# Query blocks of a PEER layer: lo parts on GpSimd, activation copies spread over the blocks, two blocks fed by the second norm

## The chip, the cores and the metric

The kernel runs on one core of a Trainium2 chip. The core's engines run side by side, each through its own list of instructions in order, and wait for each other by semaphores: PE (TensorE) multiplies matrices, DVE (VectorE) and ACT (ScalarE) work element by element, POOL (GpSimd) so far only issues row gathers, and SP issues most of the other DMAs. The metric is the time of one execution on the device, in microseconds.

## The reference

One layer of a decoder block on 512 tokens of 1024 numbers, in float32. The change lies between the second norm and the search for experts:

```python
h2 = modulate(rmsnorm(x, norm2_g[l]), shift2, scale2)
x = x + gate2[:, None, :] * peer(h2, peer_wq[l], peer_subkeys[l], peer_u[l], peer_v[l])

def peer(h, wq, subkeys, u_tab, v_tab):
    xt = h.reshape(T, D)
    q = (xt @ wq).reshape(T, PEER_HEADS, 2, PEER_HALF)               # 16 blocks of 128 columns
    sc = jnp.einsum('thpd,hpkd->thpk', q, subkeys)
    vals, ids = lax.top_k(sc, PEER_TOPK)                             # 16 of 128
    ...                                                              # 16 of 256 sums, softmax
    u = jnp.take(u_tab, ic, axis=0); a = jnp.einsum('chkd,cd->chk', u, xc)
    wgt = gc * jax.nn.gelu(a)
    vv = jnp.take(v_tab, ic, axis=0); return jnp.einsum('chkd,chk->cd', vv, wgt)
```

## The kernel before

**Products in three parts.** A float32 matrix is split into hi, a rounded copy that ACT writes (line 176), and lo, the rest, which DVE writes as raw minus hi (line 177, `split`). A product is three matmuls a piece of 128 rows: hi by hi, hi by lo, lo by hi (lines 200 to 202, `mm3`); the third is the first that reads the weights' lo. A block of weights is 128 by 1024 numbers, so a block is 8 pieces and 24 matmuls. `weights_of` loads a block (`raw`, 5 buffers), and splits it; hi and lo have 4 buffers each, so the hi of block n+4 waits until PE has read that of block n.

**The second norm** gives its result in eight pieces (line 230 on ACT: fH, lines 229 and 231 on DVE: f and fL). Ahead of it x is turned by PE and written away in eight DMAs (line 536, `x1s<-xn`; three buffers for xn). The first query block, `early`, takes each piece as it comes. Then f is turned by 16 transposes (line 593) and copied out (hN and h2N, line 595), and ACT copies fH and fL, 352 columns of each piece, to h2H and h2L, 16 copies (line 598). h2H and h2L are what the dense blocks multiply with.

**Query blocks** 0 to 15: `query(hp)` multiplies and copies the result to qs (line 735); `scores(hp)` multiplies qs with the subkeys (line 742, psc), copies that to scd (line 744), and DVE takes the sixteen largest (`level1`, lines 631 to 636, three groups of tokens); after each second block also those of the sums (`level2`, lines 642 to 655). On PE the scores of block n stand behind the matmuls of block n+1.

**Dense blocks**, `first()`: u for 128 experts times all tokens (pa), 24 matmuls of 352 columns, with lo parts on DVE. They are called between the steps of `lookup`, where DVE turns found places into expert numbers (eq), and then between the steps of `build`, where it spreads the gates (B, line 946) for PE (gps, line 954).

The order on each engine is set when the program is built: a scheduling layer turns the calls into one list an engine. A tile's buffers and the semaphores follow from the pools.

Of the kernel before, what the change touches and what calls it, by code (L numbers as in the profile page):

```python
# [7 lines left out]
F32 = mybir.dt.float32  # L8
# [5 lines left out]
AF = mybir.ActivationFunctionType  # L14
# [8 lines left out]
DC = 8  # L23
# [3 lines left out]
TU = TD - HT  # L27
# [8 lines left out]
RING = 3  # L36
LOOK = 3
SPILL = 68
EARLY = 1
STB = 2  # L40
LD = 5
AHEAD = 7
# [47 lines left out]
def body(tc, p):  # L90
    nc = tc.nc
# [18 lines left out]
    def bank(name):  # L110
        return psm.tile([P, 512], F32, tag="m", name=name)
# [55 lines left out]
    mark = [None]  # L167

    def after(ins, mark):

        if mark is not None:
            tc.add_manual_dep(ins.ins, mark.ins.name, mybir.DependencyInfo(
                mybir.DependencyClass.Sync, mybir.DependencyReason.DATA), reason="pace")

    def split(h, l, f):
        nc.scalar.activation(h, f, AF.Copy)  # L176
        nc.vector.tensor_sub(l, f, h.bitcast(F32))  # L177

    def load(src):
        raw = ld.tile([P, D], F32, tag="ld", bufs=LD, name="raw")  # L180
        nc.sync.dma_start(raw, src)
        return raw

    def parts(src):

        raw = load(src)
        h = hl.tile([P, D], F32R, tag="h", bufs=4, name="hi")
        l = hl.tile([P, D], F32R, tag="l", bufs=4, name="lo")
        split(h, l, raw)
        return h, l  # L190

    def weights_of(src):

        h, l = parts(src.rearrange("p a b -> p (a b)"))
        return (lambda k: h[:, k * P:(k + 1) * P]), (lambda k: l[:, k * P:(k + 1) * P])

    def mm3(ps, w, rh, rl, ks=range(DC), k0=0, k1=DC - 1):
        wh, wl = w
        for k in ks:
            nc.tensor.matmul(ps, wh(k), rh(k), start=(k == k0), stop=False)  # L200
            nc.tensor.matmul(ps, wh(k), rl(k), start=False, stop=False)  # L201
            mark[0] = nc.tensor.matmul(ps, wl(k), rh(k), start=False, stop=(k == k1))  # L202
# [13 lines left out]
    def tmp(name):  # L216
        return tp.tile([P, T], F32, name=name, **T2)
# [59 lines left out]
    def some_weights(m):  # L277
        for b, w in zip(FIRST, WHEN):
            if w == m:
                wj[b] = weights_of(p["w_in"][b])  # L280

    some_weights(-1)
    for m, k in enumerate(ORDER):
        if k < DC - NR:
            ada((k, 8 + k))
        else:
            ps = ada_rows(m)
            for q in range(2):
                pick = rt.tile([P, P], F32, tag="pick", name="pick", bufs=1)
                nc.vector.scalar_tensor_tensor(pick, ps[:, q, :], 1.0, ident, op0=OP.mult, op1=OP.mult,  # L290
                                               accum_out=modv[:, q, k:k + 1])
        nc.vector.tensor_add(modv[:, 0:2, k], modv[:, 0:2, k], adabv[:, 0:2, k])
        nc.vector.scalar_tensor_tensor(s1[:, k:k + 1], mod[:, 8 + k:9 + k], 1.0, S("n1g", k), op0=OP.add, op1=OP.mult)
        f = tmp("f")
        nc.vector.tensor_mul(f, xT[:, k, :], r1)
        nc.scalar.activation(f, f, AF.Identity, scale=s1[:, k:k + 1], bias=mod[:, k:k + 1])
        split(hH[:, k, :], hL[:, k, :], f)
        some_weights(m)
        if m == 4:
            nc.sync.dma_start(cs2, p["cst"][:, KEEP:])  # L300
# [35 lines left out]
    def proj(b):  # L336
        w = weights_of(p["w_in"][b])
        ps = bank("pj")
        mm3(ps, w, hh, hlo)
        return ps  # L340
# [122 lines left out]
    def part_norm(ss, src, g, o):  # L463
        r = rstd(ss, 512)
        for k in range(4):
            f = tmp("f")
            nc.vector.scalar_tensor_tensor(f, src[:, k, :], S(g, k), r, op0=OP.mult, op1=OP.mult)
            split(mH[:, o + k, :], mL[:, o + k, :], f)
# [4 lines left out]
    def out_half(b, half):  # L473
        if half == 0:
            wo[b] = weights_of(p["w_out"][b])
            py[b] = bank("py")
        mm3(py[b], wo[b], mh, ml, range(4 * half, 4 * half + 4))
# [50 lines left out]
    def spill(half, when):  # L528
        for c in range(NCH):
            ps = bank("xt")  # L530
            for i in range(4):
                after(nc.tensor.transpose(ps[:, i * P:(i + 1) * P], xT[:, 4 * half + i, c * P:(c + 1) * P], ident),
                      when)
            xn = rt.tile([P, 512], F32, name="xn", **R2)
            nc.scalar.activation(xn, ps, AF.Copy)
            nc.sync.dma_start(x1s[c][:, half * 512:(half + 1) * 512], xn)
# [22 lines left out]
    h2H = pp.tile([P, DC, TU], F32R, name="h2H")  # L559
    h2L = pp.tile([P, DC, TU], F32R, name="h2L")  # L560
# [12 lines left out]
    fH = hx.tile([P, DC, T], F32R, name="fH")  # L573
    fL = hx.tile([P, DC, T], F32R, name="fL")
    r2 = rstd(ss2, D)
    spill(0, end)
    spill(1, end)
    early = [(weights_of(p["wq"][b]), bank("pq")) for b in range(EARLY)]
    fs = []
# [4 lines left out]
    for r, (dst, cs) in enumerate(((hN, slice(TD - P, TD)), (h2N, slice(TD, T)))):  # L584
        pg = [bank("pg0"), bank("pg1")]
        for k in range(DC):
            b = mod[:, 24 + k:25 + k]
            f = fs[k]
# [4 lines left out]
            nc.tensor.transpose(pg[k // 4][:, (k % 4) * P:(k % 4 + 1) * P], f[:, cs], ident)  # L593
        for k in range(2):
            nc.scalar.activation(dst[:, k * 512:(k + 1) * 512], pg[k], AF.Copy)
    for k in range(DC):
        for d, x in ((h2H, fH), (h2L, fL)):
            nc.scalar.activation(d[:, k, :], x[:, k, 0:TU].bitcast(F32), AF.Copy)

    xp_s.close()  # L600
    tp_s.close()
    r4, r4_s = pool("r4", side="right")
# [26 lines left out]
    def level1(sc, v, ids, mark=None):  # L629

        after(nc.vector.max(v[:, 0:8], sc), mark)
        nc.vector.max_index(ids[:, 0:8], v[:, 0:8], sc)
        rest = rt.tile([P, P], F32, tag="rest", name="rest", bufs=2)
        nc.vector.match_replace(rest, v[:, 0:8], sc, -3e38)
        nc.vector.max(v[:, 8:16], rest)
        nc.vector.max_index(ids[:, 8:16], v[:, 8:16], rest)  # L636

    def level2(h, n, R):

        cand = R["pool"].tile([P, n, 112], F32, tag=f"cand{n}", name="cand", bufs=1)  # L640
        V = R["V"][:, :, h]
        nc.vector.tensor_add(cand[:, :, 0:64].rearrange("p c (a b) -> p c a b", a=4),
                             V[:, :, 0, 0:4, None].to_broadcast([P, n, 4, 16]),
                             V[:, :, 1, None, :].to_broadcast([P, n, 4, 16]))
        nc.vector.tensor_add(cand[:, :, 64:112].rearrange("p c (a b) -> p c a b", a=12),
                             V[:, :, 0, 4:16, None].to_broadcast([P, n, 12, 4]),
                             V[:, :, 1, None, 0:4].to_broadcast([P, n, 12, 4]))
        pos = R["pos"]
        for c in range(n):
            v0, v1 = R["v"][:, c, h, 0:8], R["v"][:, c, h, 8:16]  # L650
            nc.vector.max(v0, cand[:, c, :])
            nc.vector.max_index(pos[:, c, h, 0:8], v0, cand[:, c, :])
            nc.vector.match_replace(cand[:, c, :], v0, cand[:, c, :], -3e38)
            nc.vector.max(v1, cand[:, c, :])
            nc.vector.max_index(pos[:, c, h, 8:16], v1, cand[:, c, :])
# [69 lines left out]
    def query(hp):  # L725
        sk = rp.tile([P, P], F32, tag="sk", name="sk", bufs=3)
        if hp < EARLY:
            ps = early[hp][1]
        else:
            w = weights_of(p["wq"][hp])  # L730
            ps = bank("pq")
            mm3(ps, w, lambda k: fH[:, k, :], lambda k: fL[:, k, :])
        nc.sync.dma_start(sk, p["sk"][hp])
        qs = tmp("qs")
        nc.scalar.activation(qs, ps, AF.Copy)
        return qs, sk

    def scores(hp, qs, sk):
        h, q = divmod(hp, 2)
        pc = bank("psc")  # L740
        for c in range(NCH):
            nc.tensor.matmul(pc[:, c * P:(c + 1) * P], qs[:, c * P:(c + 1) * P], sk, start=True, stop=True)
        sc = tmp("scd")[:, 0:TD].rearrange("p (c k) -> p c k", c=ND)
        nc.scalar.activation(sc, pc[:, 0:TD].rearrange("p (c k) -> p c k", c=ND), AF.Copy)
        nc.scalar.activation(scg[hp // 8][:, hp % 8, :], pc[:, TD:T], AF.Copy)
        for c in range(ND):
            level1(sc[:, c, :], Rd["V"][:, c, h, q], Rd["I"][:, c, h, q])
        if q:
            level2(h, ND, Rd)

    last = None
    for hp in range(16):
        now = query(hp)
        if last:
            scores(hp - 1, *last)
        last = now
    scores(15, *last)
    weights(ND, Rd)
# [373 lines left out]
```

## Time and profile before

| what | us |
|---|---|
| three runs | 1451.26, 1445.46, 1447.48; median 1447.48 |
| the profiled execution: its time, its span | 1445.51, 1443.6 |
| PE busy, DVE busy | 1391.7 (96%), 1242.0 (86%) |
| ACT busy, POOL busy | 616.1 (43%), 411.4 (29%) |

The span runs from the first to the last instruction of the profile; times of places are counted from its start. The time holds 1.9 us beside the span. The second norm lies at 230 to 252 us, the query blocks' matmuls at 240 to 350, the choice of their largest sums until 372, the first gates at 455. A row of the timeline reads: start, length, engine, line, operation, tile written from tiles read, sizes, count, and in brackets the engine's idle time before it and what ended that. The length of a pipelined instruction is longer than its step to the next.

### The profile page before, as it was taken

The numbers are of one execution on the slowest core, as the hardware profiler recorded it, in microseconds if no ns is written. First come the engines' busy times: TensorE is split into PE (matmuls) and PEld (weight loads), VectorE is DVE, ScalarE is ACT, GpSimd is POOL, SyncE is SP. The second block draws the span as 40 slices with busy tenths as digits, with TensorE's granted clock in tenths as the row PEclk, the third lists the DMA queues.
The fourth block names the chain that finished last, engine by engine and source line by source line (L and its number), as shares of the span: only waits on it lengthen the run. The fifth ranks groups of instructions, "written<-read, shape, count | busy, mean of one in ns | idle before, by whom it ended". The sixth has DMA issues, their size and how long they took to land.

```text
span 1443.6 us, 21238 instructions
## 1 busy us (share of the span) xinstructions
PE 1391.7 (96%) x7696; PEld 1222.1 (85%) x7696; DVE 1242.0 (86%) x2267; ACT 616.1 (43%) x1041; POOL 411.4 (29%) x292
## 2 busy tenths in 40 slices
PE   6999998999897999999999999999999999999998
PEld 4776776788897999999888888889999999889997
DVE  7778978799989999998668888888789988898964
ACT  4534646423633555464433434343343324333431
POOL 0000000000032330511034444446545546565400
PEclk9999999999998999999999999999999999999999
DMA  8645535222496997898999999999999999999843
GB/s 282 226 164 166 202 124 188 82 85 89 151 305 200 382 377 280 327 384 325 364 332 362 409 395 378 396 357 380 355 362 394 388 357 343 363 343 393 319 146 131
DMA packets 134377, 418.80 MB, mean 290 GB/s; under 512 B 12801, under 2 KB 39553, under 8 KB 132737
## 3 DMA queue, kind: packets, MB, share of 16 engines
q1 hardware_dynamic: 92800, 266.45, 51.1%
q0 software_dynamic: 41472, 151.01, 27.7%
q8 instruction: 60, 0.98, 0.3%
q14 instruction: 45, 0.36, 0.1%
HBM read 375.77 MB, written 41.62 MB: 289 GB/s over the span
## 4 chain that ended last, share of the span: by engine, by line
PE 63%; DVE 24%; DMA 5%; issue 5%; ACT 2%; POOL 1%; SPq 0%; DVEq 0%; ACTq 0%; POOLq 0%
PE o L997 11%; PE o L996 11%; PE o L998 11%; PE pa L200 6%; PE pa L202 6%; PE pa L201 6%; DVE lo L177 4%; DVE junk L213 2%; DVE B L946 2%; DVE junk L784 1%; PE py L200 1%; PE py L201 1%; DVE I L636 1%; PE py L202 1%; POOL row L776 1%
## 5 line engine op out<-in xcount | busy, mean ns | idle before, releaser
L176 ACT ACTIVATE hi<-raw 128x1024 fp32r<-128x1024 f32 x298 | 312.2, 1054 | 308.2 <-PE pa L201 71.7
L177 DVE TENSOR_TENSOR lo<-raw,hi 128x1024 fp32r<-128x1024 f32 x298 | 363.2, 1221 | 42.4 <-ACT hi L176 42.0
L202 PE MATMUL pa<-h2H,lo 128*128 128x352 f32 x1024 | 330.5, 323 | 8.2 <-DVE lo L177 8.2
L200 PE MATMUL pa<-h2H,hi 128*128 128x352 f32 x1024 | 332.9, 325 | 1.4 <-ACT sp L624 1.4
L201 PE MATMUL pa<-h2L,hi 128*128 128x352 f32 x1024 | 329.5, 322 | 0.0
L997 PE MATMUL o<-lo,wwh 128*128 128x512 f32 x768 | 299.2, 390 | 0.9 <-DVE lo L177 0.9
L996 PE MATMUL o<-hi,wwh 128*128 128x512 f32 x768 | 299.6, 390 | 0.0
L998 PE MATMUL o<-hi,wwl 128*128 128x512 f32 x768 | 298.8, 389 | 0.0
L776 POOL DMA_INDIRECT row<-in_uR,eG x128 | 187.4, 1464 | 319.5 <-PE o L998 181.8
L776 POOL DMA_INDIRECT row<-in_vL,eG x128 | 179.8, 1405 | 135.4 <-PE o L998 68.6
L784 DVE SCALAR_TENSOR_TENSOR junk<-row,h2N 128x1024 bf16<-128x1024 f32 x128 | 154.2, 1224 | 63.0 <-DMA row<-in_uR,eG 62.8
L202 PEld LDWEIGHTS pa<-h2H,lo 128*128 128x128 f32 x1024 | 193.2, 189 | 9.4 <-DVE lo L177 9.4
L200 PEld LDWEIGHTS pa<-h2H,hi 128*128 128x128 f32 x1024 | 192.7, 188 | 3.7 <-ACT sp L624 1.5
L201 PEld LDWEIGHTS pa<-h2L,hi 128*128 128x128 f32 x1024 | 193.1, 189 | 2.2
L912 DVE SCALAR_TENSOR_TENSOR ga<-row,av,ga 128x1024 f32<-128x1024 f32 x127 | 163.1, 1284 | 29.7 <-DMA row<-in_vL,eG 22.0
L776 POOL DMA_INDIRECT row<-in_uR,eH x32 | 44.0, 1376 | 493.2 <-DVE eq L695 402.9
L998 PEld LDWEIGHTS o<-hi,wwl 128*128 128x128 f32 x768 | 144.2, 188 | 30.3
L997 PEld LDWEIGHTS o<-lo,wwh 128*128 128x128 f32 x768 | 144.2, 188 | 29.3 <-DVE lo L177 1.5
L996 PEld LDWEIGHTS o<-hi,wwh 128*128 128x128 f32 x768 | 144.1, 188 | 28.3 <-issue 0.2
L176 ACT ACTIVATE wwh<-w 128x768 fp32r<-128x768 f32 x64 | 54.2, 846 | 164.0 <-DVE w L979 118.0
L978 ACT ACTIVATE w<-G 128x32 f32<-128x32 f32 x128 | 22.3, 221 | 190.4 <-DVE wwl L177 179.9
L177 DVE TENSOR_TENSOR wwl<-w,wwh 128x768 fp32r<-128x768 f32 x64 | 61.1, 955 | 9.8 <-ACT wwh L176 9.8
(265 smaller groups left out, 1852.0 us busy)
## 6 DMA issues: line engine op xcount, KB each, us to landing
raw<-in_uL SPq DMA_DIRECT2D x128, 512.0 KB
raw<-in_vL SPq DMA_DIRECT2D x128, 512.0 KB
Gd<-st SPq DMA_DIRECT2D x12, 2048.0 KB
G<-Gd SPq DMA_DIRECT2D x16, 1536.0 KB
ada<-in_ada SPq DMA_DIRECT2D x32, 512.0 KB
Ad<-sp SPq DMA_DIRECT2D x34, 352.0 KB
sp<-Ad SPq DMA_DIRECT2D x34, 352.0 KB
raw<-in_w_in SPq DMA_DIRECT2D x18, 512.0 KB
```

The source lines that it names most:

```text
L176: nc.scalar.activation(h, f, AF.Copy)
L177: nc.vector.tensor_sub(l, f, h.bitcast(F32))
L200: nc.tensor.matmul(ps, wh(k), rh(k), start=(k == k0), stop=False)
L201: nc.tensor.matmul(ps, wh(k), rl(k), start=False, stop=False)
L202: mark[0] = nc.tensor.matmul(ps, wl(k), rh(k), start=False, stop=(k == k1))
L213: nc.vector.scalar_tensor_tensor(junk, raw, 1.0, cact, op0=OP.mult, op1=OP.mult, accum_out=mod[:, b:b + 1])
L776: d = nc.gpsimd.indirect_dma_start(out=t, out_offset=None, in_=tab, in_offset=bass.IndirectOffsetOnAxis(ap=e, axis=0))
L784: return nc.vector.scalar_tensor_tensor(junk, t, 1.0, h, op0=OP.mult, op1=OP.mult, accum_out=a)
L912: nc.vector.scalar_tensor_tensor(ga, t, av[:, k:k + 1], ga, op0=OP.mult, op1=OP.add)
L996: nc.tensor.matmul(o, wh[:, cs], vh[:, hs], start=(j == 0), stop=False)
L997: nc.tensor.matmul(o, wh[:, cs], vl[:, hs], start=False, stop=False)
L998: last = nc.tensor.matmul(o, wl[:, cs], vh[:, hs], start=False, stop=(j == NJ - 1))
```

## The change

`split`, `parts` and `weights_of` take the engine of the subtraction, and `query` passes GpSimd. EARLY goes from 1 to 2: the first two query blocks follow the norm piece by piece, with their lo parts still on DVE. So fourteen lo parts, those of blocks 2 to 15, stand on GpSimd. The 16 copies to h2H and h2L leave their place behind the norm; two stand in each of the loop's steps 2 to 9, behind the scores of the block before, with a dependence on the last matmul of the query block before.

```diff
-EARLY = 1
+EARLY = 2
-    def split(h, l, f):
+    def split(h, l, f, by=nc.vector):
         nc.scalar.activation(h, f, AF.Copy)
-        nc.vector.tensor_sub(l, f, h.bitcast(F32))
+        by.tensor_sub(l, f, h.bitcast(F32))
...
-    for k in range(DC):
-        for d, x in ((h2H, fH), (h2L, fL)):
-            nc.scalar.activation(d[:, k, :], x[:, k, 0:TU].bitcast(F32), AF.Copy)
-
...
-            w = weights_of(p["wq"][hp])
+            w = weights_of(p["wq"][hp], nc.gpsimd)
...
     for hp in range(16):
+        so_far = mark[0]
         now = query(hp)
         if last:
             scores(hp - 1, *last)
+            if 2 <= hp < 2 + DC:
+                for d, x in ((h2H, fH), (h2L, fL)):
+                    after(nc.scalar.activation(d[:, hp - 2, :], x[:, hp - 2, 0:TU].bitcast(F32), AF.Copy), so_far)
         last = now
```

PE's list at the start of query block 2, before (pq_2129 is block 1, psc_2157 the scores of block 0, pq_2190 block 2; in brackets whose semaphores an instruction waits for):

```order
L202 MATMUL pq_2129<-fH_1912,lo_2126 128x512
L742 MATMUL psc_2157<-sk_2118,qs_2120 128x128 [waits DMAHW3_49,PE_49,Activation_49]
L742 MATMUL psc_2157<-sk_2118,qs_2120 128x128 x3
L200 MATMUL pq_2190<-fH_1912,hi_2186 128x512 [waits PE_49]
L201 MATMUL pq_2190<-fL_1913,hi_2186 128x512
L202 MATMUL pq_2190<-fH_1912,lo_2187 128x512
```

The same place now (pq_1994 is block 1, pg1_2104 the last of the transposes' four targets, psc_2141 the scores of block 0, pq_2174 block 2):

```order
L202 MATMUL pq_1994<-fH_1912,lo_1991 128x512
L593 MATMUL pg0_2075<-cst_83,f_1995 128x128 [waits PE_49]
...
L593 MATMUL pg1_2104<-cst_83,f_2065 128x128
L738 MATMUL psc_2141<-sk_2133,qs_2135 128x128 [waits DMAHW3_49,Activation_49]
L738 MATMUL psc_2141<-sk_2133,qs_2135 128x128 x3
L200 MATMUL pq_2174<-fH_1912,hi_2170 128x512 [waits Activation_49]
L201 MATMUL pq_2174<-fL_1913,hi_2170 128x512
L202 MATMUL pq_2174<-fH_1912,lo_2171 128x512 [waits Pool_49]
```

The 16 transposes stood among the matmuls of the first two blocks and now stand behind all 48 of them; block 2's lo is waited for from POOL.

ACT's list where the copies to h2H and h2L end, before:

```order
L598 ACTIVATE h2H<-fH 128x352
L598 ACTIVATE h2L<-fL 128x352
L735 ACTIVATE qs<-pq 128x512 x2
L176 ACTIVATE hi<-raw 128x1024
L744 ACTIVATE scd<-psc 128x384
L745 ACTIVATE scg_2116<-psc 128x128
L176 ACTIVATE hi<-raw 128x1024 x2
```

ACT's list behind the norm now (line 592 is the norm's last piece of work on ACT):

```order
L592 ACTIVATE f<-f,mod 128x160 x2
L176 ACTIVATE hi<-raw 128x1024
L731 ACTIVATE qs<-pq 128x512
L595 ACTIVATE hN<-pg_2075 128x512
L595 ACTIVATE hN<-pg_2076 128x512
L595 ACTIVATE h2N<-pg_2103 128x512
L595 ACTIVATE h2N<-pg_2104 128x512
L731 ACTIVATE qs<-pq 128x512
L740 ACTIVATE scd<-psc 128x384
L741 ACTIVATE scg_2131<-psc 128x128
L755 ACTIVATE h2H<-fH 128x352
L755 ACTIVATE h2L<-fL 128x352
```

The qs of block 0 stood behind 16 copies and now stands behind one hi; the first two copies follow the scores of block 0.

SP's list at the end of the norm's loads, before (the two last raw tiles are those of query blocks 7 and 8):

```order
L181 DMA raw_2543<-in_wq 128x1024 [waits DVE_49]
L181 DMA raw_2604<-in_wq 128x1024 [waits DMAHW3_49,DVE_49]
L536 DMA x1s_1651<-xn_1922 128x512 [waits Activation_49]
L536 DMA x1s_1651<-xn_1930 128x512 [waits DMAHW4_49,Activation_49]
L536 DMA x1s_1651<-xn_1938 128x512 [waits DMAHW5_49,Activation_49]
```

The same place now:

```order
L181 DMA raw_2537<-in_wq 128x1024 [waits Pool_49]
L181 DMA raw_2600<-in_wq 128x1024 [waits DMAHW3_49,Pool_49]
L536 DMA x1s_1651<-xn_1922 128x512 [waits Activation_49]
L536 DMA x1s_1651<-xn_1930 128x512 [waits DMAHW4_49,Activation_49]
L536 DMA x1s_1651<-xn_1938 128x512 [waits DMAHW5_49,Activation_49]
```

The order is the same; the two loads, whose buffers are those of blocks 2 and 3, wait for POOL's subtraction where they waited for DVE's.

## Rows read from the trace of the kernel before

**Rows 1.** Busy time by stage (windows).

```profile
core 0: us, PE busy (x) PEld busy (x) DVE busy (x) ACT busy (x) POOL busy (x), PEclk, DMA share, GB/s
260.00:350.00 90.00, 90.00 (x442) 75.65 (x441) 86.89 (x483) 29.16 (x56) 0.00 (x0) 0.98 0.29 92
440.00:460.00 20.00, 12.21 (x85) 11.86 (x84) 20.00 (x60) 6.85 (x11) 4.01 (x3) 0.79 0.66 204
...
260.00:270.00 10.00, 10.00 (x44) 8.21 (x43) 7.70 (x31) 4.07 (x8) 0.00 (x0) 0.83 0.39 120
270.00:280.00 10.00, 10.00 (x49) 8.36 (x48) 9.93 (x62) 2.10 (x5) 0.00 (x0) 1.00 0.34 110
```

**Rows 2.** PE's waits, 225 to 480 us: total, times, longest.

```profile
PE gps L954 <- DVE B L946: 6.9, 1, 6.9
PE pa L202 <- DVE lo L177: 4.9, 2, 3.2
PE psc L742 <- ACT qs L735: 3.2, 2, 2.6
PE pq L200 <- ACT fH L230: 3.0, 1, 3.0
```

**Rows 3.** Timeline of PE, from the norm to the last query block.

```profile
240.13 0.79 PE L200 MATMUL pq<-fH,hi 128*128 128x512 f32 x1 [3.00 <-ACT fH L230]
...
249.82 0.93 PE L593 MATMUL pg<-cst,f 128*128 128x128 f32 x7
...
256.08 0.40 PE L202 MATMUL pq<-fH,lo 128*128 128x512 f32 x1
259.13 1.16 PE L742 MATMUL psc<-sk,qs 128*128 128x128 f32 x8 [2.65 <-ACT qs L735]
260.04 0.48 PE L200 MATMUL pq<-fH,hi 128*128 128x512 f32 x1
...
267.22 1.05 PE L742 MATMUL psc<-sk,qs 128*128 128x128 f32 x8
268.03 0.48 PE L200 MATMUL pq<-fH,hi 128*128 128x512 f32 x1
...
350.42 1.05 PE L742 MATMUL psc<-sk,qs 128*128 128x128 f32 x8
```

**Rows 4.** ACT: the copies' group (ns, starts), and its timeline.

```profile
L598 ACT ACTIVATE h2H<-fH x8: 504/512/514, 251.3 to 257.7; 128x352 fp32r<-128x352 f32 x8
...
258.47 1.08 ACT L735 ACTIVATE qs<-pq 128x512 f32<-128x512 f32 x2
...
343.99 1.06 ACT L176 ACTIVATE hi<-raw 128x1024 fp32r<-128x1024 f32 x1 [4.31 <-PE pq L201]
```

**Rows 5.** Timeline of DVE, query blocks: lo parts, a level1's start, the last level2.

```profile
289.57 1.21 DVE L177 TENSOR_TENSOR lo<-raw,hi 128x1024 fp32r<-128x1024 f32 x1
...
303.11 1.22 DVE L177 TENSOR_TENSOR lo<-raw,hi 128x1024 fp32r<-128x1024 f32 x1
...
349.60 1.21 DVE L177 TENSOR_TENSOR lo<-raw,hi 128x1024 fp32r<-128x1024 f32 x1
350.72 0.48 DVE L631 MAX8 V<-scd 128x8 f32<-128x128 f32 x2
...
371.75 0.27 DVE L655 FIND_INDEX8 pos<-Rv,cand 128x8 uint32<-128x112 f32 x1
```

**Rows 6.** Ahead of the norm: ACT's hi, SP's load, ACT's wait (timeline).

```profile
230.86 1.06 ACT L176 ACTIVATE hi<-raw 128x1024 fp32r<-128x1024 f32 x1 [1.46 <-PE py L201]
...
233.20 0.33 SPq L181 DMA_DIRECT2D raw<-in_wq  x1
...
238.25 1.21 ACT L535 ACTIVATE xn<-xt 128x512 f32<-128x512 f32 x2 [2.44 <-DMA x1s<-xn]
```

**Rows 7.** Groups of POOL over the span (count, busy us, mean ns).

```profile
L776 POOL DMA_INDIRECT row<-in_uR,eG x128 | 187.4, 1464 | 319.5 <-PE o L998 181.8
```

**Rows 8.** A group of DVE, 262 to 350 us: instructions with two inputs.

```profile
L642 DVE TENSOR_TENSOR cand<-V 128x192 f32<-128x192 f32 x6 | 2.0, 340 | 0.0
```

More of the change, by code (lines that the diff above doesn't have):

```diff
@@ L182, in load, with parts @@
         return raw
-    def parts(src):
+    def parts(src, by=nc.vector):
         raw = load(src)
@@ L188, in parts, with weights_of @@
         l = hl.tile([P, D], F32R, tag="l", bufs=4, name="lo")
-        split(h, l, raw)
+        split(h, l, raw, by)
         return h, l
-    def weights_of(src):
-        h, l = parts(src.rearrange("p a b -> p (a b)"))
+    def weights_of(src, by=nc.vector):
+        h, l = parts(src.rearrange("p a b -> p (a b)"), by)
         return (lambda k: h[:, k * P:(k + 1) * P]), (lambda k: l[:, k * P:(k + 1) * P])
```

## Prediction

> **What bounds the kernel now.** I read the stages first [rows 1]. From 260 to 350 us, while the query blocks run, PE and DVE both look full (90.00 and 86.89 of 90 us) and POOL does nothing. From 440 to 460 PE is busy for 12.21 of 20 us and DVE for all of it. Two engines that both look full are told apart by their periods. The scores of a block stand on PE at 267.22 and, thirteen blocks later, at 350.42 [rows 3]: 6.40 us a block, 12.80 a pair. DVE repeats itself in pairs, because a level2 follows each second block: its lo parts at 289.57 and 303.11 are one pair apart, 13.54 us [rows 5]. So in this stage DVE is the slower engine by 0.74 us a pair, and PE runs ahead of it. How far behind DVE is at the end is seen at the lo part of dense block 2: its hi is there at 343.99 + 1.06 = 345.05 [rows 4], but DVE comes to it at 349.60 [rows 5], 4.55 us late. The last level2 ends at 372, some 20 us after the last scores on PE.
>
> Then I read what PE waits for between 225 and 480 us [rows 2]: 3.0 us for the first piece of the norm, 2.6 for the first qs, 4.9 in two pieces for lo parts of dense blocks, 6.9 for the first gates (B). The first two are the norm's; the last two are DVE's lateness, which is handed on through the lookup. After 460 PE is nearly always busy, so what is gained at 455 should stay to the end, and no more.
>
> **The first query blocks.** Before, block 1 ends near 256.3, PE waits 2.65 us for a qs that stands behind sixteen copies on ACT, and block 2 starts at 260.04 [rows 3]. The h2H copies, with the h2L copies between them, start from 251.3 to 257.7, and qs starts at 258.47 [rows 4]. Block 2 takes 7.18 us until its scores (260.04 to 267.22); later blocks take 6.40 less the scores' 0.81 (267.22 to 268.03), so 5.59. The granted clock was 0.83 in those ten microseconds and 1.00 in the next [rows 1]: PE came back from its wait at the lower level (1.2 GHz) for a part of the block, and that cost 1.59 us.
>
> Now the first 48 matmuls run from 240.13 without waiting for much else: 48 times 5.59/24 is 11.18, and I add the same 1.59 for the low clock at their start, since PE waits 3.0 us ahead of them. The 16 transposes behind them cost 0.93/7 = 0.13 each, 2.1 together. PE is at the scores of block 0 at 255.0 and at block 2 at 255.8. Block 0's qs is ready by then: its matmuls end some 0.7 us before block 1's (252.9), and one hi and one qs (1.06 and about 0.6) make it 253.9. Block 2 thus starts 4.2 us earlier, and keeps the high clock, 1.6: PE leads by **5.8**. The copies, some 0.4 us apart (eight pairs and a little else in 6.4 us), lie in ACT's idle time of 4.31 us a block [rows 4]; were it not there, a block would grow by 0.8.
>
> **What the move to GpSimd costs.** No row shows arithmetic on POOL. From below, its subtraction costs DVE's 1.22 us [rows 5]; the nearest row of POOL itself is a gather's issue, 1.46 us [rows 7]; from above I take the period of a block, 6.40, for beyond it PE would wait for every block. Up to there block n+4's lo has three blocks' time, 19 us. I take 1.9, half as long again as DVE. The Trainium skill gives a price (GPSIMD Engine Reference, section 3.1: a two-input addition of 2048 float32 numbers takes 1.96 times DVE's time); that would be an estimate of 2.4 us here and make the sum 8.5 in place of 9.0.
>
> One place is not covered. SP issues its DMAs in order, and the load of block 8, ahead of the eight `x1s` DMAs, now waits for POOL's subtraction of block 3. Its hi ends at 230.86 + 1.06 = 231.92, and the load went out at 233.20 [rows 6], 1.28 later. With 1.9 it goes out 0.6 later; the `x1s` DMAs share the DMA engines with it, ACT waits for the first of them (2.44 us, at 238.25), and the norm's first piece stands behind that on ACT. So I take off **0.6** (nothing at 1.22, 5.1 at 6.40). PE's lead is 5.2.
>
> **What DVE gains.** Fourteen lo parts leave DVE, of 1.12 us each by the step from 349.60 to 350.72 [rows 5]. A pair then takes 13.54 - 2.24 = 11.30 us, less than PE's 12.80: DVE waits for PE, and the lateness of 4.55 goes, less one pair's 0.74, since the lo parts of dense blocks 0 to 2 stay on DVE in the last blocks. The other DVE savings are worth nothing: they become waits for scores. From dense block 2 on, DVE stands at 5.2 + 4.55 - 0.74 = **9.0** us earlier.
>
> **What follows.** PE reaches the dense blocks 5.2 earlier, and would save its two waits of 4.9 for lo parts, together 10.1; but those lo parts are only 9.0 earlier, so some 1.1 of waiting is left, and both engines stand 9.0 earlier. The gathers of the lookup follow DVE's numbers and move with them. The order of PE, DVE and ACT after the query blocks is as before, so both engines arrive 9.0 earlier at the first gates, and the wait of 6.9 stays. I find nothing behind it that changes. Sum: 9.0 us. From the profiled execution's own time that is 1445.51 - 9.0 = 1436.5 (span 1434.6, and 1.9 around it); that execution is 2.0 us under the median of 1447.48, which would give 1438.5. I put the prediction between them: **1437.5**.
>
> **Rivals.** *Only PE's lead counts* (0.20). If dense blocks' hi on ACT, the gathers or the lookup hold DVE back, its 9.0 shrinks to PE's 5.2: 1441.3. For it speaks that ACT carries the lookup's copies too; against it that each of these follows DVE or PE, which are both early.
>
> *The gates come early too* (0.10). If DVE gets through the lookup with fewer waits, PE's 6.9 at 455 goes as well: 1430.6. Against it: DVE had no idle time from 440 to 460 [rows 1], so it has to win all of it before.
>
> *POOL stops DVE* (0.08, slower). If DVE stood still whenever POOL subtracts, a block would cost DVE 6.77 - 1.12 + c. Twelve lo parts (blocks 4 to 15) lie inside the stage, so DVE loses 12 times (c - 1.12) against before and has 3.6 to spend (4.2 - 0.6): it decides at c = 1.4. At c = 2.5 the loss is 13 us, 1459. No row shows POOL's arithmetic beside DVE's, so nothing in the trace excludes it.
>
> *Only two-input instructions wait* (0.05, about level or slower). In a pair DVE has two such, the sums for level2 (0.34 us and one like it) [rows 8]. If each always waited a whole subtraction, a pair would lose 3.8 where 1.5 are free, 2.3 net, over five pairs 11: 1448.5. But POOL is busy 1.9 of 6.4 us, so such a wait would come to some 0.3 times half of 1.9, 0.6 a pair, within the free 1.5, and the forecast would stand. The Trainium skill has this rule (SBUF — State Buffer, section Who interferes with whom: a DVE instruction with two SBUF inputs contends with a GpSimd instruction that reads SBUF, and one with a single input does not). By that rule the rival before this one would not occur, since level1 and most of level2 read one input; no run here shows it yet.
>
> *POOL is slower than a block* (0.04). At 8 us a subtraction, PE would lose 1.6 on each of fourteen blocks, 22 us, and the norm would start 6.7 later: about 1468. It decides near 6.4.
>
> **Chances.** The forecast has 0.53. Its own range, 1434 to 1441, comes from POOL's price (1.22 to about 3 us), from the low clock's cost at the start, and from the spread of the runs. The whole range, 1430 to 1445, takes in the first two rivals and leaves out the others. About 0.5%, 7 us, is what a measurement of this kernel can tell from no change; the runs shown lie 5.8 apart. Faster by more than that: most of the forecast and the early gates, 0.62. Within it: the rest of the forecast, PE's lead alone and part of the two-input case, 0.26. Slower: 0.12.
>
> **What would show it.** In the changed profile block 2 should start near 256.4 with the clock at 1.00 after it; POOL should show fourteen subtractions near 1.9 us; DVE should show idle time waiting for scd in the query blocks, and lo of dense block 2 within 1 us of its hi; the last level2 should end near 363; the waits for dense lo parts should sum to about 1; B should still be waited for some 7 us, near 446. The prediction is wrong if level1's instructions grow longer beside POOL's, if PE waits for POOL, if `x1s` goes out several microseconds later, or if the lead at the first gates is not that at the last level2.

## Result and profile after

The changed kernel takes 1437.88 us (median of 8 runs, 1436.58 to 1443.21) where the kernel before took 1447.60 beside it (8 runs): ratio 0.9944, 95% interval 0.9924 to 0.9964. In a later comparison it took 1435.71 (6 runs) against 1446.00, ratio 0.9919 (0.9889 to 0.9948). The ratios are not those of the medians, which would be 0.9933 and 0.9929. The forecast was 1437.5.

The profiled execution took 1436.58 us, its span 1434.8. Windows of it, with the columns of [rows 1]:

```profile
core 0: us, PE busy (x) PEld busy (x) DVE busy (x) ACT busy (x) POOL busy (x), PEclk, DMA share, GB/s
240.00:250.00 10.00, 8.21 (x35) 6.43 (x36) 9.56 (x15) 9.97 (x23) 0.00 (x0) 1.00 0.37 141
250.00:260.00 10.00, 10.00 (x58) 8.62 (x57) 3.89 (x22) 8.38 (x19) 3.57 (x2) 1.00 0.28 80
260.00:350.00 90.00, 89.44 (x457) 76.02 (x456) 81.77 (x503) 35.34 (x72) 25.26 (x11) 1.00 0.30 92
```

From 260 to 350 us DVE is no longer full (81.77 of 90, before 86.89), and POOL works for 25. The granted clock is 1.00 in all three; before, it was 0.83 in the ten microseconds from block 2 on. PE's waits from 225 to 480 us, to be held against [rows 2]:

```profile
PE gps L954 <- DVE B L946: 7.0, 1, 7.0
PE pq L200 <- ACT fH L230: 3.0, 1, 3.0
PE ss L551 <- DVE sq L223: 1.4, 1, 1.4
PE pa L202 <- DVE lo L177: 1.4, 1, 1.4
PE gps L955 <- DVE B L946: 0.9, 1, 0.9
PE psc L738 <- ACT qs L731: 0.6, 1, 0.6
```

The wait for qs went from 3.2 to 0.6, that for dense lo parts from 4.9 to 1.4; that for B stayed. One is new: ss waits 1.4 for DVE, ahead of the norm. The timeline of PE (the last py matmul, the norm's first, block 2, the scores of block 14), against [rows 3]:

```profile
230.93 0.39 PE L202 MATMUL py<-mH,lo 128*128 128x512 f32 x1
...
241.74 0.73 PE L200 MATMUL pq<-fH,hi 128*128 128x512 f32 x2 [3.04 <-ACT fH L230]
...
254.93 1.06 PE L738 MATMUL psc<-sk,qs 128*128 128x128 f32 x8
255.75 0.48 PE L200 MATMUL pq<-fH,hi 128*128 128x512 f32 x1
...
344.54 0.60 PE L738 MATMUL psc<-sk,qs 128*128 128x128 f32 x4
```

And DVE, POOL and ACT: first the place ahead of the norm, then lo of dense block 2, the last level2 and B ([rows 4, 5, 6] hold most of the same rows before).

```profile
226.02 1.22 DVE L177 TENSOR_TENSOR lo<-raw,hi 128x1024 fp32r<-128x1024 f32 x1
227.16 2.36 DVE L554 SCALAR_TENSOR_TENSOR s<-mod,sm 128x8 f32<-128x8 f32 x1
229.44 1.21 DVE L177 TENSOR_TENSOR lo<-raw,hi 128x1024 fp32r<-128x1024 f32 x1
...
340.01 1.21 DVE L177 TENSOR_TENSOR lo<-raw,hi 128x1024 fp32r<-128x1024 f32 x1
...
362.16 0.27 DVE L651 FIND_INDEX8 pos<-Rv,cand 128x8 uint32<-128x112 f32 x1
...
443.34 1.27 DVE L946 TENSOR_TENSOR B<-H,L 128x2048 f16<-128x2048 f16 x1
```

```profile
226.89 2.60 POOL L177 TENSOR_TENSOR lo<-raw,hi 128x1024 fp32r<-128x1024 f32 x1 [226.44 <-ACT hi L176]
233.00 2.35 POOL L177 TENSOR_TENSOR lo<-raw,hi 128x1024 fp32r<-128x1024 f32 x1 [3.51 <-ACT hi L176]
...
275.29 2.40 POOL L177 TENSOR_TENSOR lo<-raw,hi 128x1024 fp32r<-128x1024 f32 x1 [4.00 <-ACT hi L176]
281.69 2.40 POOL L177 TENSOR_TENSOR lo<-raw,hi 128x1024 fp32r<-128x1024 f32 x1 [4.00 <-ACT hi L176]
```

```profile
239.85 1.23 ACT L535 ACTIVATE xn<-xt 128x512 f32<-128x512 f32 x2 [2.46 <-DMA x1s<-xn]
240.97 0.71 ACT L230 ACTIVATE fH<-f,mod 128x512 fp32r<-128x512 f32 x1
...
338.16 1.06 ACT L176 ACTIVATE hi<-raw 128x1024 fp32r<-128x1024 f32 x1 [4.31 <-issue]
```

hi of dense block 2 ends at 339.22 and its lo starts 0.8 later: DVE's lateness of 4.55 is gone. The last level2 ends at 362.4 (before 372.0) and B starts at 443.34 (before 453.60 by the same view). The product of 8 columns on DVE (L554), 0.17 us long before, takes 2.36 while POOL's first subtraction runs beside it.

**A common origin.** Over the fourteen profiles of this study, PE's last py matmul starts between 226.97 and 233.03 us, and from B to the end it takes 987.6 to 996.8, with no order by kernel. Places are therefore counted from the start of the last py matmul, as 241.74 - 230.93 = 10.81 for the norm's first matmul here:

| kernel | norm on PE | block 2 | last level2 ends | B |
|---|---|---|---|---|
| before | 9.52 | 29.43 | 141.4 | 223.0 |
| the change | 10.81 | 24.82 | 131.5 | 212.4 |
| the change, second profile (after_again) | 10.47 | 26.87 | 133.6 | 215.5 |
| gps_only | 11.13 | 32.07 | 139.7 | 220.6 |
| dve_lo | 9.07 | 24.75 | 135.2 | 216.8 |
| copies_old | 10.94 | 33.16 | 141.3 | 222.1 |
| one_early | 10.92 | 28.07 | 134.8 | 217.0 |
| lo23_dve | 8.86 | 24.76 | 131.4 | 212.8 |
| lo2_dve | 10.69 | 27.22 | 133.9 | 214.9 |
| lo3_dve | 9.06 | 24.37 | 131.1 | 211.9 |
| triple | 9.05 | 24.48 | 144.0 | 224.9 |
| dense5_pool | 9.85 | 24.89 | 128.8 | 214.1 |
| lo23_warm | 9.91 | 23.92 | 130.6 | 211.8 |
| dense5_warm | 9.01 | 23.18 | 127.1 | 211.8 |

### The profile page after: what moved, and what is told of

It reads as the page before. It is cut to its first block, busy times and chain, and to the rows that moved or that the text cites. A ratio compares the mean times of both kernels' runs of the same rounds, so it can differ in the third digit from the quotient of the medians.

```text
span 1434.8 us, 21241 instructions
## 1 busy us (share of the span) xinstructions
PE 1385.5 (97%) x7696; PEld 1218.7 (85%) x7696; DVE 1229.3 (86%) x2253; ACT 616.0 (43%) x1041; POOL 442.7 (31%) x306
## 4 chain that ended last, share of the span: by engine, by line
PE 62%; DVE 20%; DMA 8%; issue 7%; POOL 1%; ACT 1%; SPq 0%; DVEq 0%; POOLq 0%; ACTq 0%
PE o L997 10%; PE o L998 10%; PE o L996 10%; PE pa L200 5%; PE pa L202 5%; PE pa L201 5%; DVE lo L177 4%; DMA row<-in_vL,eG 3%; DMA ada<-in_ada 2%; PE pq L202 2%; PE pq L201 2%; PE pq L200 2%; DVE B L946 2%; DVE ga L912 2%; PE pj L200 2%
## 5 line engine op out<-in xcount | busy, mean ns | idle before, releaser
L177 DVE TENSOR_TENSOR lo<-raw,hi 128x1024 fp32r<-128x1024 f32 x284 | 345.2, 1218 | 31.9 <-ACT hi L176 31.1
L177 POOL TENSOR_TENSOR lo<-raw,hi 128x1024 fp32r<-128x1024 f32 x14 | 33.8, 2413 | 288.3 <-ACT hi L176 288.3
## 6 DMA issues: line engine op xcount, KB each, us to landing
G<-Gd SPq DMA_DIRECT2D x16, 1536.0 KB, 12.5
```

The source lines that it names most:

```text
L177: by.tensor_sub(l, f, h.bitcast(F32))
```

## Experiments

**What each part is worth.** The theory is that of the prediction: spreading the copies and the second early block give PE a lead, GpSimd lets DVE follow it. Four kernels leave out one part, or two.

gps_only: one early block, the copies in their old place, lo parts on GpSimd.

```diff
-EARLY = 2
+EARLY = 1
...
-            if 2 <= hp < 2 + DC:
-                for d, x in ((h2H, fH), (h2L, fL)):
-                    after(nc.scalar.activation(d[:, hp - 2, :], x[:, hp - 2, 0:TU].bitcast(F32), AF.Copy), so_far)
```

(with the three lines of before put back behind the norm)

> Of the change only the move of the lo parts to GpSimd: one early query block, the sixteen copies in their old place, lo of query blocks 1 to 15 on GpSimd. Theory (GpSimd takes DVE's lateness away and gives PE nothing): the norm starts some 1.3 us later because one subtraction on GpSimd holds up DVE ahead of it, so block 2 starts near 261.5 and PE is at the scores of block 14 near 352, 1.5 us later than before; DVE is on time there, with lo of dense block 2 within 1 us of its hi, near 347.3 (before 349.60); 2 to 2.5 us faster in all, ratio 0.998. Rival A (GpSimd's part is the larger one): 4 us or more faster. Rival B (without PE's lead the lo parts on GpSimd win nothing): 0 to 1.5 us slower.

Measured: ratio 0.9981 (0.9964 to 0.9999). Block 2 starts 2.6 us later than before, the scores of block 14 (350.41 - 228.62 = 121.79, before 119.81) 2.0 later, and lo of dense block 2 stands 0.8 behind its hi; the last level2 ends 1.7 earlier, B 2.4. The theory holds, within about 1 us at each place. Rival B falls by the ratio. Rival A (4 us or more) lies within the ratio's interval, which reaches from 0.1 to 5.2 us, and falls only by the 2.4 at B.

dve_lo: everything but GpSimd.

```diff
-            w = weights_of(p["wq"][hp], nc.gpsimd)
+            w = weights_of(p["wq"][hp])
```

> The change without the move to GpSimd: two early blocks, copies spread, every lo on DVE. Theory: the norm starts as before (240.1 on PE), block 2 starts between 254.1 and 255.7, PE leads by 6 to 7.5 us at the scores of block 14, but DVE is the slower engine as before and its lead is only that of its first level1, 5 to 6 us, so lo of dense block 2 stands near 344 and again several us behind its hi; 5 to 6 us faster, ratio 0.996. Rival (PE's lead is worth nothing while DVE is the slower engine): under 2 us faster.

Measured: PE leads by 6.3 us at the scores of block 14, lo of dense block 2 is 4.6 behind its hi again, PE waits 4.7 for dense lo parts, and the last level2 and B come 6.2 earlier. The rows of dense block 2 on ACT and DVE:

```profile
337.51 1.06 ACT L176 ACTIVATE hi<-raw 128x1024 fp32r<-128x1024 f32 x1 [4.31 <-PE pq L201]
...
343.14 1.21 DVE L177 TENSOR_TENSOR lo<-raw,hi 128x1024 fp32r<-128x1024 f32 x1
```

The profile has the theory's sizes. The time has not: the ratio, 0.9985 (0.9969 to 1.0002), leaves out the expected 0.996 and doesn't exclude the rival's gain of under 2 us, though the medians, 1441.70 and 1446.21, are 4.5 apart. Why the 6.2 us at B are not all in the time is not shown.

copies_old: two early blocks and GpSimd, the copies in their old place.

> The change with the sixteen copies back in their old place (two early blocks, lo on GpSimd). Theory (the copies are what held qs up): qs of blocks 0 and 1 stand behind all sixteen copies on ACT, PE waits for qs 4 us or more, block 2 starts near 261.5 with a low clock after it; PE's lead is gone and what is left is DVE's lateness, 2 to 2.5 us faster than before, ratio 0.998. Rival (two early blocks are what brings PE its lead): block 2 near 256, ratio 0.994 as with the whole change.

Its edit is the second half of gps_only's. Measured: ratio 0.9993 (0.9975 to 1.0011). PE waits 5.5 us for qs, and block 2 starts 3.7 later than before, more than the theory's 1.5. Nothing of PE's lead is left; the rival falls.

```profile
PE gps L954 <- DVE B L946: 6.1, 1, 6.1
PE psc L741 <- ACT qs L734: 6.1, 2, 5.5
```

These are copies_old's longest waits on PE. With both early blocks done by then, PE has nothing else to do behind the copies.

one_early: EARLY is 1, the rest as in the change.

> The change with one early block instead of two (copies spread, lo on GpSimd). Theory: PE's matmuls of blocks 0 and 1 take 16.3 us from the norm's first piece as they did before, in place of 14.0; block 2 starts near 259.0 without a wait for qs and at the full clock; PE leads by 2.6 us at the scores of block 14, DVE by 6.4 at dense block 2; ratio 0.9956. Rival (spreading the copies does it all): block 2 near 256, ratio 0.994 as with the whole change.

Measured: ratio 0.9961 (0.9943 to 0.9979); block 2 28.07 after the origin, 1.4 earlier than before, the scores of block 14 3.0 earlier, the last level2 6.7. The theory holds: the second early block is worth what the first 48 matmuls and 16 transposes gain, 17.2 us here against 14.0 to 16.5.

Left out one by one, the parts cost B a lead of 10.6 us as follows: the copies 9.7, the second early block 4.6, GpSimd 4.3 (by the change's first profile). Measured from the second profile, whose lead is 7.5, they are 6.6, 1.5 and 1.3. So the copies are the largest part by both, and the order of the other two is not shown: two profiles of one program differ by 3.1 us at B.

**What delays the norm.** In the change, the norm reached PE 1.3 us later than before. Two suspects: DVE's instruction held up by POOL (L554), and SP's queue, as the prediction had it.

lo23_dve: lo of blocks 2 and 3 on DVE, so POOL does nothing ahead of the norm.

```diff
-            w = weights_of(p["wq"][hp], nc.gpsimd)
+            w = weights_of(p["wq"][hp], nc.vector if hp < 4 else nc.gpsimd)
```

> The whole change, but lo of query blocks 2 and 3 stay on DVE, so that GpSimd does nothing ahead of the norm. From PE's last py matmul to its first fH matmul it is 9.3 us before and 10.6 with the change. Theory (GpSimd's subtractions ahead of the norm delay it, and nothing later does): this falls to 9 to 9.3 us, the scores of block 14 stand 7.5 to 7.9 us earlier than before by the same origin (with the change 6.2), dense lo parts are still on time, and the first gates B stand 11.8 to 12.3 us earlier (with the change 10.6); 1 to 1.5 us faster than the change, ratio to before 0.993. Rival (the later start of the norm was the spread of the runs): 10.6 us stays and nothing is won.

Measured: ratio 0.9946 (0.9930 to 0.9963). The norm comes at 8.86, no later than expected, but block 2 stands at 24.76 as in the change, and against the change's first profile nothing is won. The expected gain was lost again in the 48 matmuls, which took 15.9 us instead of 14.0. Windows of lo23_dve:

```profile
240.00:250.00 10.00, 9.16 (x32) 7.07 (x33) 9.56 (x15) 10.00 (x25) 0.00 (x0) 0.83 0.39 144
250.00:260.00 10.00, 10.00 (x58) 8.62 (x57) 2.51 (x17) 7.34 (x16) 2.95 (x2) 1.00 0.22 68
```

The clock was at the low level for a part of the first ten microseconds, as before the change.

lo2_dve (`hp == 2` in the same line) and lo3_dve (`hp == 3`) leave one of the two subtractions on POOL.

> The whole change, but lo of query block 2 alone stays on DVE; lo of block 3 is GpSimd's, ahead of the norm, and SP's load of block 8, with the x1s behind it, still waits for it. Theory (what delays the norm is a DVE instruction with two inputs that is held up by the subtraction of block 2): last py to first fH matmul 9 to 9.4 us, and the product of x and ss on DVE (scalar_tensor_tensor of 8 columns) near 0.2 us instead of 2.4. Rival A (SP's queue, as the prediction had it): 10 us or more, with the load of block 8 again some 3.5 us later than before. Rival B (the subtraction of block 3 holds up another DVE instruction): 10 us or more, with some DVE instruction 2 us longer near 233 to 236.

> The whole change, but lo of query block 3 stays on DVE, so that SP's load of block 8 waits for no GpSimd work, while lo of block 2 is GpSimd's. It tells whether the held-up DVE instruction alone is enough. Theory (either of two delays is enough, and in the change they lie beside each other: DVE held up by the subtraction of block 2, SP's queue by that of block 3): the product of 8 columns on DVE takes 2 us or more again, ACT's wait for the x1s DMA is 2 to 2.8 us, and from the last py matmul to the first fH matmul it is 10.4 to 10.9 us (with neither, in four runs, 8.9 to 9.9; with both 10.8). Rival (SP's queue is all of it): 9 to 9.9 us.

Measured, one time each: 1437.46 and 1433.87 us. In lo2_dve L554 takes 0.16 us, and yet the norm comes at 10.69: ACT waits longer for the `x1s` DMA (before 2.44, [rows 6]), which SP issues behind the load that waits for POOL.

```profile
237.79 1.23 ACT L535 ACTIVATE xn<-xt 128x512 f32<-128x512 f32 x2 [3.59 <-DMA x1s<-xn]
238.92 0.71 ACT L230 ACTIVATE fH<-f,mod 128x512 fp32r<-128x512 f32 x1
```

That is the prediction's own mechanism (rival A), worth 3.59 - 2.44 = 1.15 us against before. The `x1s` DMAs go out when they did before, 4.26 us after the origin, but 0.50 us behind the load in place of 1.67. In the eight profiles that have the 1.67, before among them, the wait is 1.80 to 2.81, so the size is known only within 0.8 to 1.8 us. In lo3_dve, L554 was not held up this time, and the norm came at 9.06. Its rows on DVE and POOL:

```profile
223.88 1.22 DVE L177 TENSOR_TENSOR lo<-raw,hi 128x1024 fp32r<-128x1024 f32 x1
225.02 0.16 DVE L554 SCALAR_TENSOR_TENSOR s<-mod,sm 128x8 f32<-128x8 f32 x1
225.09 1.22 DVE L177 TENSOR_TENSOR lo<-raw,hi 128x1024 fp32r<-128x1024 f32 x1
...
227.67 1.45 DVE L223 TENSOR_TENSOR sq<-sq 128x512 f32<-128x512 f32 x1 [0.70 <-ACT sq L221]
```

```profile
225.19 3.39 POOL L177 TENSOR_TENSOR lo<-raw,hi 128x1024 fp32r<-128x1024 f32 x1 [224.73 <-DVE lo L177]
```

Here POOL came 0.1 us after DVE's next subtraction had begun, and it was POOL that took 1 us longer. On DVE only sq was held up, by 0.76 us (0.69 before), and DVE waited for PE behind it all the same. (In gps_only and one_early it is one of DVE's own subtractions that takes 3.42 us in place of 1.22, ahead of the norm.) So lo3_dve doesn't tell whether a held-up L554 alone delays the norm, and its theory is not shown by it. gps_only shows a delay by DVE alone, there of a subtraction: its load goes out 2.29 us ahead of `x1s`, more than the 1.67 before, and ACT's wait for `x1s` is short,

```profile
237.75 1.30 ACT L535 ACTIVATE xn<-xt 128x512 f32<-128x512 f32 x2 [0.99 <-DMA x1s<-xn]
```

yet rstd (line 241 on ACT, which the norm's pieces need) comes 2.41 us later than before and the norm 1.61.

after_again: the change unaltered, for a second profile.

> The changed kernel once more, as the control of lo23_warm and for the granted clock in the 48 first matmuls. In its profile those ran at the full clock throughout and took 14.0 us until block 2; without GpSimd work ahead of the norm they took 15.0 to 15.9, with the low clock for some microseconds. Theory A (the low clock comes or not by chance of the run): block 2 starts 24.5 to 26.5 us after the last py matmul, with some stretch at the low clock this time. Theory B (the change's own timing keeps the clock up): 24.7 to 24.9 again, clock 1.00 from 240 to 250.

Its rows on DVE, ACT and POOL:

```profile
227.83 0.16 DVE L554 SCALAR_TENSOR_TENSOR s<-mod,sm 128x8 f32<-128x8 f32 x1
227.91 1.22 DVE L177 TENSOR_TENSOR lo<-raw,hi 128x1024 fp32r<-128x1024 f32 x1
```

```profile
240.55 1.20 ACT L535 ACTIVATE xn<-xt 128x512 f32<-128x512 f32 x2 [3.40 <-DMA x1s<-xn]
```

```profile
227.90 3.48 POOL L177 TENSOR_TENSOR lo<-raw,hi 128x1024 fp32r<-128x1024 f32 x1 [227.44 <-ACT hi L176]
```

The same program, and this time POOL is held up and L554 is not; DVE's sq takes 1.45 as in lo3_dve, and rstd is not late (3.07 after the origin, before 3.06). The norm is late by SP's queue (3.40 against 2.44; `x1s` goes out 0.51 behind the load), 0.95 in all. In the first profile it was late by DVE (rstd 1.25 later by the origin: 235.24 - 230.93 = 4.31 against 3.06) with the usual wait for `x1s`. Either way it costs about 1 us, and the two did not add up. Theory A holds for the clock: block 2 at 26.87, a little beyond the expected 26.5, the clock at 0.60 from 242 to 250, 16.4 us for the 48 matmuls.

```profile
242.00:250.00 8.00, 7.59 (x21) 5.94 (x22) 7.59 (x12) 8.00 (x20) 0.00 (x0) 0.60 0.43 164
```

lo23_warm: as lo23_dve, with nine more matmuls in PE's pause ahead of the norm; the first fH matmul overwrites what they write.

```diff
-    fs = []
+    fs = [nc.tensor.matmul(early[0][1], early[0][0][0](i % DC), hot[0][:, 0:512], start=True, stop=True) for i in range(9)][9:]
```

(`hot[0]` is the hi part of block 0)

> As lo23_dve (lo of blocks 2 and 3 on DVE), with nine extra matmuls of 512 columns on PE between the last transposes of x and the first fH matmul; their result is overwritten. In lo23_dve the norm came 1.6 to 1.9 us earlier than with the change, but PE's clock fell to the low level at the first matmuls and block 2 started no earlier (24.75 us after the last py matmul, with the change 24.8). Theory (PE's pause ahead of the norm is what costs the clock): the clock stays at 1.00 from 240 to 250, block 2 starts 22.8 to 23.3 us after the last py matmul, and B comes 1.5 to 2 us earlier than in lo23_dve; ratio to before 0.9935. Rival A (the low clock comes whatever PE did in the pause): block 2 near 24.7 again. Rival B (the clock is not what bounds these 48 matmuls; DVE's pieces of the norm are): the clock is full, block 2 stays near 24.5.

Its PE timeline (L579 are the added matmuls) and windows:

```profile
236.23 2.31 PE L579 MATMUL pq<-hi 128*128 128x512 f32 x9
239.87 0.73 PE L200 MATMUL pq<-fH,hi 128*128 128x512 f32 x2 [1.34 <-ACT fH L230]
```

```profile
240.00:250.00 10.00, 9.94 (x43) 7.82 (x44) 8.64 (x13) 9.97 (x26) 0.00 (x0) 1.00 0.36 130
```

The clock stays at the high level, and the 48 matmuls take 14.0 us: the theory on the clock holds, and rivals A and B fall. Block 2 stands at 23.92, later than the 22.8 to 23.3 expected, because the norm itself came at 9.91 (ACT waited 2.81 for `x1s`, in lo23_dve 1.80, with nothing on POOL). B is 1.0 us earlier than in lo23_dve, where 1.5 to 2 was expected. Ratio 0.9930 (0.9910 to 0.9950), not told apart from lo23_dve's.

**How much POOL can take.** triple: as lo23_dve, each of POOL's twelve subtractions is done three times.

```diff
-        by.tensor_sub(l, f, h.bitcast(F32))
+        for _ in range(3 if by is nc.gpsimd else 1): by.tensor_sub(l, f, h.bitcast(F32))
```

> As lo23_dve, but GpSimd makes each of its twelve subtractions three times over (7.2 us where a block has 6.40 us). Theory (a lo part has three blocks' time, 19 us, before PE needs it, so a lag of 0.8 us a block, 9 us at block 15, stays within it): PE waits for no GpSimd lo, the scores of block 14 stand where lo23_dve has them within 1 us. The prediction's rule (it decides near the period of a block): 8 to 10 us later. Third theory (GpSimd that is always busy holds up DVE's instructions with two inputs, the sums for level2): those take 2 us or more on average, and DVE falls behind PE, with lo of dense block 2 several us behind its hi.

Measured, one time: 1448.83 us; lo23_dve 1437.17. Groups of DVE from 262 to 342 us, in triple and then in lo23_dve (count, busy us, mean ns, idle before):

```profile
L638 DVE TENSOR_TENSOR cand<-V 128x192 f32<-128x192 f32 x5 | 9.8, 1961 | 0.0
L641 DVE TENSOR_TENSOR cand<-V 128x144 f32<-128x144 f32 x5 | 9.0, 1795 | 0.0
L627 DVE MAX8 V<-scd 128x8 f32<-128x128 f32 x32 | 8.5, 280 | 2.5 <-ACT scd L740 2.5
```

```profile
L627 DVE MAX8 V<-scd 128x8 f32<-128x128 f32 x38 | 10.1, 282 | 6.6 <-ACT scd L740 6.6
...
L638 DVE TENSOR_TENSOR cand<-V 128x192 f32<-128x192 f32 x6 | 2.0, 338 | 0.0
L641 DVE TENSOR_TENSOR cand<-V 128x144 f32<-128x144 f32 x6 | 1.8, 302 | 0.0
```

With POOL always busy (78.27 of these 80 us) the two sums take 3.1 us more in a pair; MAX8, with one input, takes what it took. The last level2 ends 12.5 later and B 12.1. The third theory holds: the two sums are just under its 2 us, and lo of dense block 2 (352.52) is 3.8 behind its hi. The first falls: PE waited 2.5 us for POOL's lo parts, and the scores of block 14 stood 3.1 later. The prediction's rule wanted 8 to 10 at those scores and falls there; the total is near it by another cause.

**More on POOL.** dense5_pool: as lo23_dve, and the first five dense blocks' lo parts on POOL.

```diff
-        w = weights_of(p["uL"][j])
+        w = weights_of(p["uL"][j], nc.gpsimd if j < 5 else nc.vector)
```

> As lo23_dve, with the lo parts of the first five dense blocks on GpSimd too. Theory (from the last scores on DVE alone sets the pace, and its largest-value instructions read one input, so GpSimd beside them costs nothing): the last level2 ends 2.2 to 4 us earlier than in lo23_dve by the same origin, PE's wait for the lo of a dense block falls to nothing, B comes 2 to 4 us earlier, and the wait for B falls to some 5 us; 2 to 4 us faster than lo23_dve, ratio to before 0.991. Rival A (the sums for level2 and the other two-input instructions of the last blocks wait for GpSimd): no gain or 1 to 3 us lost at the end of level2. Rival B (B is set by something else than DVE's work): B unmoved.

Measured: ratio 0.9907 (0.9891 to 0.9924), median 1432.27. The last level2 ends 2.6 us earlier than in lo23_dve, as expected. B comes 1.3 later, and PE waits 1.4 for a dense lo and 8.6 for B; the total is the theory's, but the picture is neither the theory's nor a rival's. Beside lo23_dve, timed with it, it is faster: the intervals 0.9891 to 0.9924 and 0.9930 to 0.9963 don't meet. DVE's list from the lookup on is in another order in this kernel, so B no longer measures the same amount of work, and where the time came from is not settled.

dense5_warm: dense5_pool and the nine matmuls of lo23_warm.

> Both parts that helped together: lo of blocks 2 and 3 on DVE, lo of the first five dense blocks on GpSimd, nine extra matmuls on PE ahead of the norm's first piece. Theory (the parts lie in different stages and add up): the clock is 1.00 from 240 to 250, the 48 matmuls take 14.0 us, the last level2 ends 127 to 128.5 us after the last py matmul (lo23_dve 131.4, dense5_pool 128.8), ratio to before 0.987 to 0.991, at or below dense5_pool's 0.9907. Rival (B stays where DVE's lookup puts it, and what PE wins ahead of it becomes its wait for B): B within 0.5 us of 214 us after the last py matmul, the wait for B 9 us or more, ratio no better than 0.9907.

Measured: the clock at 1.00, 14.2 us for the 48 matmuls, the last level2 at 127.1, as the theory has it; B at 211.8, so the rival falls by its own number, though PE waits 8.6 for B. The ratio, 0.9934 (0.9914 to 0.9955), is not below dense5_pool's and misses the theory's 0.987 to 0.991. The medians of the two (1432.27 and 1433.74) are the lowest of the study, but the intervals touch or overlap that of the change; no version is shown to beat it.

## Why the prediction was right, step by step

**Total and DVE's gain.** The sum was 9.0 us from the last level2 on. By the common origin it is 9.9 there and 10.6 at B in the first profile, 7.9 and 7.5 in the second; the medians are 9.7 and 10.3 us lower. The steps of DVE hold as worked out: DVE's lateness of 4.55 became 0.8, DVE waits for scd in the query blocks (6.6 us from 262 to 340), dense lo parts are waited for 1.4 us (1.1 forecast), and the wait for B stayed at 7.0. dve_lo and gps_only show the two halves apart: PE's lead without POOL leaves DVE as late as before, and POOL without PE's lead saves 2.4. That the lead at B is handed on to the end is not shown by the profiles, since the stretch behind B takes 987.6 to 996.8 us in them; the medians agree with it for the change, and dve_lo's ratio does not bear it out.

That the median lies 0.4 us from the forecast is luck. The intervals of the two comparisons allow a gain of 5 to 16 us, the two profiles differ by 3.1 us at B, and two terms of PE's lead were mis-sized, which in the first profile cancel in part (1.7 us better and 0.7 worse than forecast).

**PE's lead** was forecast at 5.8 less 0.6. Measured at the scores of block 14: 119.81 - 113.61 = 6.2 in the first profile, 4.1 in the second (347.61 - 231.94 = 115.67). Both terms in it were mis-sized. *The 48 matmuls with their transposes and scores*, forecast at 15.7 with 1.59 for the low clock, took 14.0 and 16.4; the eight profiles with both early blocks, the copies spread and no added matmuls range from 14.0 to 16.5, and the two with nine matmuls in the pause took 14.0 and 14.2. The assumption of one low-clock stretch was right for the usual execution and wrong for the first profile. *The norm's delay*, forecast at 0.6, measured 1.3 and 0.95 against the one profile of before (9.52 from the origin; the seven profiles without POOL's work ahead of the norm, this one among them, have 8.86 to 9.91). Its mechanism, SP's load behind POOL's subtraction, is shown by lo2_dve and the second profile; the size was low because POOL's price was: with 2.41 in place of 1.9, the step's own working (2.41 less 1.28) gives 1.1, near the 1.15 of lo2_dve. The delay by DVE in the first profile was missing from the working.

**POOL's price** was taken at 1.9 us; it is 2.41, 1.98 times DVE's 1.22. POOL's group in the changed kernel:

```profile
L177 POOL TENSOR_TENSOR lo<-raw,hi 128x1024 fp32r<-128x1024 f32 x14 | 33.8, 2413 | 288.3 <-ACT hi L176 288.3
```

The Trainium skill's factor (GPSIMD Engine Reference, section 3.1) was the better estimate: 1.96 times 1.22 is 2.4. In the query stage the difference cost nothing, as argued from the three blocks' time: PE never waits for POOL's lo there.

**The rivals.** *Only PE's lead counts* falls by both profiles: PE leads by 6.2 and 4.1 us, and B comes 10.6 and 7.5 earlier. *The gates come early too* falls, since the wait for B stayed, 7.0 and 7.4. *POOL is slower than a block* doesn't arise at 2.41 us; its price, about 1468, comes to 1466 by its own terms (1437.5 + 22.4 + 6.7 - 0.6). *POOL stops DVE* is excluded: MAX8 took 280 ns in triple, where POOL never rested, and 282 in lo23_dve. *Only two-input instructions wait* is the right mechanism: triple shows it at the rival's place, the sums for level2, at 3.1 us a pair. That triple's one run, 1448.83, comes so near the rival's price of 1448.5 is chance, as triple keeps POOL busy with three subtractions a block. The Trainium skill's rule (SBUF — State Buffer, section Who interferes with whom), which for instructions with one input holds outside DVE's two-port modes, agrees with these numbers: 338 and 302 ns became 1961 and 1795, MAX8 stayed. What failed was the prediction's estimate of how often it comes, 0.3 by chance. In the changed kernel it came ahead of the norm (L554), which the rival had not, and never came in the query blocks (the two sums take at most 340 and 302 ns), because POOL's subtractions and DVE's sums are both paced by PE's blocks. The sums on DVE's timeline:

```profile
279.18 0.30 DVE L641 TENSOR_TENSOR cand<-V 128x144 f32<-128x144 f32 x1
280.00 0.34 DVE L638 TENSOR_TENSOR cand<-V 128x192 f32<-128x192 f32 x1
291.98 0.30 DVE L641 TENSOR_TENSOR cand<-V 128x144 f32<-128x144 f32 x1
```

They start 1.5 us after POOL's subtraction of 275.29 has ended and are done 1.3 us before that of 281.69; the next pair is 12.80 later, as POOL's is. By these rows, as an estimate, a subtraction of up to some 3.9 us would have met none of them.

## What to carry to other kernels

When work goes to GpSimd, list DVE's instructions with two inputs in the same stretch and see whether a common pace keeps them apart; the average share of POOL's time doesn't answer that. When a part gives one engine a lead, look for the engine that must follow it: here GpSimd alone was worth 2.4 us at B, two of the three parts together 0.9 to 6.2, and leaving out the copies alone cost nearly all. Time what comes out of a profile from an event that the kernels share, and take two profiles before a term of a microsecond is believed.

## What the runs showed of the hardware

A two-input DVE instruction of 0.17 us took 2.36 beside a subtraction on POOL, and in another execution of the same program POOL's subtraction took 3.48 instead of 2.4 while DVE's ran its usual 1.22; which engine is held up depended on some 0.1 us of arrival. Where POOL's subtraction began 0.06 or 0.07 us ahead of DVE's (one_early, gps_only), DVE's took 3.42; where it began 0.01 ahead or 0.10 behind (after_again, lo3_dve), POOL's took 3.48 and 3.39. The granted clock after PE's pause ahead of the norm was 1.00 in one execution of the changed kernel, and 0.50 from 242 to 248 us in another; nine matmuls in the pause kept it at 1.00 in both kernels that had them.
